# Single blocks moved ahead of the seven-product blocks in a feed-forward trunk on one core

## The chip, the core and the metric

The kernel runs on one core of a Trainium2 chip. A core has four compute engines that matter here, each with its own queue worked in order: TensorE (PE in the profile; the loads of its stationary operand are listed as PEld), VectorE (DVE), ScalarE (ACT) and GpSimd (POOL). SyncE (SP) issues DMAs, and POOL issues some too. Matmul results go to PSUM, which has eight banks here, each 128 partitions by 512 fp32 values.

The metric is the device time of one execution in microseconds (us). Before the change it was 1024.64, the median of three runs (1024.53 to 1025.91).

## The reference

A trunk of two layers on x of 256 tokens by 1024 features, all in fp32. Each layer has a feed-forward network (FFN), a mixer and a second FFN, each added to a scaled x and followed by a layer norm:

```python
D_MODEL, SEQ, DEPTH, D_FF = 1024, 256, 2, 2816

def swiglu_ffn(x, w_in, w_out):
    gate, up = jnp.split(x @ w_in, 2, axis=-1)
    return (jax.nn.silu(gate) * up) @ w_out

# layer i:
#   x <- LN(a*x + 0.5*SwiGLU_1(x))
#   x <- LN(a*x + Mixer_{i mod 2}(x))     mixer 0: sparse attention, mixer 1: Mamba-2 SSD
#   x <- LN(a*x + 0.5*SwiGLU_2(x))
```

The change concerns the four FFNs. In the profiled execution the first runs from about 10 to 190 us, the second from 288 to 465, the third from 465 to 640 and the fourth from 833 to 1021; attention and the SSD mixer lie between.

## The kernel before

**Weights.** The weights lie in DRAM in units of 128 x 1024 fp32 values. Class `Weights` brings each through four steps. SP loads it into a buffer `raw` (L240). ACT casts it to `wh`, a form that PE multiplies fast but with fewer bits (L321, in `make`). DVE subtracts it from `raw` to give `wl`, the low half (L349, in `lows`). PE then forms each product from three matmuls, high by high, low by high and high by low (`mm3`, L527 to L529). Some units are sums of two units: DVE adds the two `raw` buffers (L288), or POOL adds them by a DMA that accumulates (L261). `sums` issues these additions, up to two units ahead of what is made. There are ten slots for made units, and `raws` (7 or 9) limits the loaded ones. `pump` makes the next units; with `most` it stops where DVE is already given much work (`debt`).

**An FFN.** The 2816 hidden columns are 22 blocks of 128, worked in three kinds of steps.

- *Wide blocks* (blocks 0 to 3, eight units): x^T times the weights, token half after token half. In the first FFN the second wide block uses the banks `ptr`, elsewhere all use the two banks `pmm`. Beside them run the eight pieces of `xT.sums` (L564 to L579), which form sums of parts of x^T on ACT (L558) and DVE.
- *Seven-product blocks* (`seven(j, outs)`, four columns each, 14 units): seven products instead of eight, in the order A11, Q1, Q4, S2, S3, A12, A22, in banks `pmm` and one `ptr`, with the output units of earlier blocks (12 matmuls into the banks `acc`) between them. Four of its units are weight sums by DVE and four by POOL.
- *Single blocks* (`one(j)`, one column each): the gate half, then the up half, each a `proj_w` of one unit: eight matmuls of 512 columns (L676) and eight of 256 (L678). ACT copies the second half of the bank out (L885), and DVE's add (L886) reads the first half, after which the bank is free. Then come silu (ACT, L896), the product (DVE, L889) and the high and low forms of the result (ACT L891, DVE L892).

For wide and seven-product blocks, `glu` forms silu and product (L772, L775, L778), and `turn` transposes the result on PE (L764, into `pht` or `ptr`); ACT (L765) and DVE (L766) take it out. At the end of an FFN `tail` runs six output units for the first 128 tokens, then for the others, and the layer norms (DVE L610, L621, L623, L630, L634; POOL L517 and L519). The next stage's transposes of x (L545) follow them.

The order on each engine is the order in which the program emits the instructions. `later(f, d)` puts a piece of work off by d steps; `step` works off these pieces and then pumps units. What stands ahead of a piece in an engine's queue is thus set by where the steps lie. `ffn_plan` names the steps of an FFN: 'S' are seven-product blocks with the output units that run in them, 'R' the single blocks, and the last list is the tail's output units.

Of the kernel before, what the change touches and what calls it, by code (L numbers as in the profile page):

```python
# [63 lines left out]
MOST = 2500  # L64


def ffn_plan():


    s = [(4, [[0], [1], [2], [3]]), (8, [[6], [7], [4], [5]]), (12, [[10], [11], [8], [9]]),  # L70
         (16, [[14], [15], [12], [13]])]
    return [('S', *a) for a in s] + [('R', 20, []), ('R', 21, [])], [16, 17, 18, 19, 20, 21]


def ffn_units(ws, wi, wo, wide):
# [125 lines left out]
class Weights:  # L201
# [158 lines left out]
            self.make()  # L360
            n -= 1

    def pump(self, n=1, now=False, most=None):


        now = now or not self.defer
        if not now:
            self.lows()
        while n and self.made < self.n and self.made < self.done + self.slots:
            if most is not None and self.debt > most and self.made > self.done + 5:  # L370
                break
            self.make()
            n -= 1
        if now:
            self.lows()
        else:
            self.sums()
# [28 lines left out]
def trunk_kernel(ctx: ExitStack, tc: tile.TileContext, widths, forms, x, ln_g, ln_b, wts, kvg, convp,  # L406
# [22 lines left out]
    def f1(s):  # L429
        return wk.tile([128, 256], F32, name=nm(s), tag="f1", bufs=6)  # L430

    def r2(s):
        return wk.tile([128, 512], F32R, name=nm(s), tag="r2", bufs=10)
# [7 lines left out]
    def pmm():  # L441
        return psum.tile([128, 512], F32, name=nm("pmm"), tag="pmm", bufs=2)
# [11 lines left out]
    def ptr():  # L454
        return psum.tile([128, 512], F32, name=nm("ptr"), tag="ptr", bufs=2)

    W = Weights(nc, f4, ring, wts, widths, forms, SLOTS, RAWS)
# [22 lines left out]
    def warm_up(n):  # L480

        for i in range(n):
            nc.tensor.transpose(warm[:, (i % 4) * 128:(i % 4 + 1) * 128], ident, ident)
# [248 lines left out]
    def ffn(xT, u0, ln_i, first=False, last=False, ff=False):  # L732
# [9 lines left out]
        def later(f, d=1):  # L742

            while len(queue) < d:
                queue.append([])
            queue[d - 1].append(f)

        def items():
            for f in queue.pop(0) if queue else []:
                f()  # L750

        def step(n=2, most=MOST):
            items()
            W.pump(n, most=most)

        ready = {}

# [10 lines left out]
        def glu(t, w, c, sil=None):  # L768


            g, h = (c[:, :256], c[:, 256:]) if sil is None else (sil, f1("h"))
            nc.scalar.activation(g, c[:, :256], AF.Silu)  # L772
            out_of = sil is not None and (w >= WIDE or (t and w and not first))
            if out_of:
                nc.scalar.copy(h, c[:, 256:])  # L775

            def mul():
                nc.vector.tensor_mul(h, h if out_of else c[:, 256:], g)  # L778
                W.owe(800)
                ready.setdefault(w, {})[t] = h  # L780
                if len(ready[w]) == 2:
                    later(lambda: later(turn(w, ready.pop(w))), 2)

            later(mul)

        def wide(t, w, ps, k0, k1):
            proj_a(ps, xT, t, u + 4 * w, 512, 2, t == 1, k0, k1)

        if first:
            W.make(between=lambda: xT.fill(0, [0]))  # L790
            warm_up(WARM)
            xT.fill(1, [0])
            for w in range(WIDE):
                ps = [ptr(), ptr()] if w else [pmm(), pmm()]
                for k in range(0, DK, 2):
                    for t in range(2):
                        if (w, k, t) == (0, 0, 1):
                            W.pump(1, now=True)
                        if (w, k) == (0, 2):
                            xT.fill(t, [1])  # L800
                            W.pump(1 + 2 * t, now=True)
                        if (w, k, t) == (0, 4, 1):
                            W.pump(3, now=True)
                        wide(t, w, ps[t], k, k + 2)
                    if w:
                        items()
                        W.pump(1, now=True)
                for t in range(2):
                    glu(t, w, ps[t], f1("sil"))
                if not w:  # L810
                    for i in range(8):
                        later(lambda i=i: xT.sums(i), 1 + i // 2)
        else:
            for t in range(2):
                for w in range(WIDE):
                    ps = pmm()
                    if t:
                        for k in range(0, DK, 2):
                            wide(t, w, ps, k, k + 2)
                            if k % 4:  # L820
                                W.product()
                            if k + 2 < DK:
                                step(1)
                            W.defer = True
                    else:
                        wide(t, w, ps, 0, 5)
                        items()
                        if w == WIDE - 1:
                            W.lows()
                            xT.fill(1)  # L830
                            for i in range(8):
                                later(lambda i=i: xT.sums(i), 1 + i)
                        wide(t, w, ps, 5, DK)
                        items()
                    glu(t, w, ps, f1("sil"))
                    if t:
                        step(1)
# [32 lines left out]
        def one(j):  # L870

            nonlocal u
            bank = pmm if j % 2 == 0 else ptr
            if j % 2 == 0:
                hH[j // 2], hL[j // 2] = r2("hH"), r2("hL")
            H, L = [a[j // 2][:, (j % 2) * 256:(j % 2 + 1) * 256] for a in (hH, hL)]
            g, h = f1("gate"), f1("h")

            def half(o):
                nonlocal u  # L880
                ps = bank()
                proj_w(ps, xT, u)
                W.product()
                u += 1
                nc.scalar.copy(o, ps[:, SEQ:])  # L885
                return lambda: nc.vector.tensor_add(o, ps[:, :SEQ], o)  # L886

            def mul():
                nc.vector.tensor_mul(h, h, g)  # L889
                W.owe(1400)  # L890
                later(lambda: nc.scalar.copy(H, h))  # L891
                later(lambda: nc.vector.tensor_sub(L, h, H.bitcast(F32)), 2)  # L892

            later(half(g))
            step(most=None)
            later(lambda: nc.scalar.activation(g, g, AF.Silu))  # L896
            later(half(h))
            later(mul, 2)
            step(most=None)

        def seven(j, outs):

# [797 lines left out]

    xT = XT(True)
    u, xT = ffn(xT, 0, 0, first=True)
    u, xT = attention(xT, u, 1)
    u, xT = ffn(xT, u, 2, ff=True)
    u, xT = ffn(xT, u, 3)
    u, xT = ssd(xT, u, 4)
    u, _ = ffn(xT, u, 5, last=True)
# [36 lines left out]
```

## Time and profile before

| | us |
|---|---|
| median of three runs | 1024.64 |
| profiled execution | 1022.81 |
| its span | 1021.1 |
| PE busy | 1004.0 (98%) |
| DVE busy | 907.6 (89%) |
| ACT busy | 661.6 (65%) |
| DVE's subtractions `wl`, L349 | 494.9 in 423 |
| ACT's casts `wh`, L321 | 429.9 in 430 |
| DVE's weight sums, L288 | 76.8 in 64 |

Busy time of PE is the time in which any matmul is in the pipe, and matmuls overlap: a matmul of 512 columns is listed with 0.39 us, though in a dense stretch one starts every 0.23. In a timeline the number in front is the start from the beginning of the span, and the second one is the duration; `x8` says that the row stands for eight instructions. What stands in brackets is idle time ahead of the instruction and what ended it.

### The profile page before, as it was taken

What the parts mean: (1) busy time and instruction counts of PE and PEld (TensorE: products, weight loads), DVE (VectorE), ACT (ScalarE), POOL (GpSimd) and SP (SyncE); (2) the same over time, 40 slices, a digit from 0 to 9 for tenths busy, and PEclk for the clock granted to TensorE, in tenths of its full rate; (3) what the DMA queues carried; (4) which work ended last, traced back from release to release, by engine and by line L of the source; (5) the groups of instructions that cost most, each with busy time, mean ns of one, the idle gap of its engine ahead of it and who ended that gap; (6) DMA issues with size and microseconds to landing.
All of it is one profiled execution on the core that took longest, in us unless ns stands there. A gap on an engine that the chain in (4) does not pass through costs nothing.

```text
span 1021.1 us, 14624 instructions
## 1 busy us (share of the span) xinstructions
PE 1004.0 (98%) x5279; PEld 847.8 (83%) x5279; DVE 907.6 (89%) x1264; ACT 661.6 (65%) x965; POOL 121.4 (12%) x179
## 2 busy tenths in 40 slices
PE   8999999999999999999999999999999999999996
PEld 7788888888787888888888888999899888888885
DVE  6899998789789999988999998788999978999985
ACT  6666775477656667764676775486876645777760
POOL 2101100100011011001110100150111110101101
PEclk9999999999999999999999999999999999999998
DMA  9899999352547899992789999358765654999861
GB/s 334 219 287 277 294 262 350 116 155 94 187 144 170 266 285 293 255 374 88 183 271 275 299 265 338 127 174 240 208 216 188 198 202 108 279 273 252 256 235 41
DMA packets 64665, 231.70 MB, mean 227 GB/s; under 512 B 7280, under 2 KB 7344, under 8 KB 64592
## 3 DMA queue, kind: packets, MB, share of 16 engines
q1 hardware_dynamic: 51264, 183.43, 49.2%
q0 software_dynamic: 13040, 46.82, 23.6%
q8 instruction: 41, 0.67, 0.3%
q10 hardware_dynamic: 288, 0.52, 0.1%
q14 instruction: 32, 0.26, 0.1%
HBM read 193.48 MB, written 1.08 MB: 191 GB/s over the span
## 4 chain that ended last, share of the span: by engine, by line
PE 79%; DVE 11%; DMA 4%; issue 3%; ACT 2%; POOL 1%; SPq 0%; POOLq 0%; DVEq 0%; ACTq 0%
PE pmm L529 10%; PE pmm L527 10%; PE pmm L528 10%; PE acc L527 9%; PE acc L529 9%; PE acc L528 9%; DVE wl L349 4%; DVE raw L288 2%; DMA raw<-raw 2%; PE pxs L527 2%; PE pxs L529 2%; PE pxs L528 2%; PE pmm L676 1%; PE ptr L676 1%; PE ptr L527 1%
## 5 line engine op out<-in xcount | busy, mean ns | idle before, releaser
L349 DVE TENSOR_TENSOR wl<-raw,wh 128x1024 fp32r<-128x1024 f32 (+2 forms) x423 | 494.9, 1212 | 11.1 <-ACT wh L321 10.3
L321 ACT CAST wh<-raw 128x1024 fp32r<-128x1024 f32 (+3 forms) x430 | 429.9, 1045 | 109.8 <-DVE raw L288 52.0
L527 PE MATMUL acc<-wh,hH 128*128 128x512 f32 (+1 forms) x352 | 137.8, 392 | 0.0
L528 PE MATMUL acc<-wl,hH 128*128 128x512 f32 (+1 forms) x352 | 136.6, 388 | 0.7 <-DVE wl L349 0.7
L529 PE MATMUL acc<-wh,hL 128*128 128x512 f32 (+1 forms) x352 | 136.8, 389 | 0.3 <-DVE hL L766 0.2
L527 PE MATMUL pmm<-wh,xT 128*128 128x512 f32 (+2 forms) x320 | 125.8, 393 | 0.0
L529 PE MATMUL pmm<-wh,xT 128*128 128x512 f32 (+2 forms) x320 | 123.4, 386 | 0.1
L528 PE MATMUL pmm<-wl,xT 128*128 128x512 f32 (+2 forms) x320 | 122.9, 384 | 0.0
L261 POOL DMA_DIRECT2D raw<-raw x64 | 55.4, 865 | 448.3 <-DVE raw L288 250.2
L528 PE MATMUL pmm<-wl,xf 128*128 128x512 f32 x256 | 100.2, 391 | 1.5 <-DVE wl L349 1.5
L527 PE MATMUL pmm<-wh,xf 128*128 128x512 f32 x256 | 100.4, 392 | 0.4
L529 PE MATMUL pmm<-wh,xf 128*128 128x512 f32 x256 | 99.8, 390 | 0.0
L529 PEld LDWEIGHTS acc<-wh,hL 128*128 128x128 f32 x352 | 66.1, 188 | 14.9 <-DVE hL L766 1.2
L528 PEld LDWEIGHTS acc<-wl,hH 128*128 128x128 f32 x352 | 66.2, 188 | 14.1 <-DVE wl L349 1.1
L288 DVE TENSOR_TENSOR raw<-raw,raw 128x1024 f32<-128x1024 f32 x64 | 76.8, 1217 | 0.2
L527 PEld LDWEIGHTS acc<-wh,hH 128*128 128x128 f32 x352 | 66.2, 188 | 12.8
L529 PEld LDWEIGHTS pmm<-wh,xT 128*128 128x128 f32 x320 | 60.2, 188 | 13.5 <-DVE xT L524 1.4
L528 PEld LDWEIGHTS pmm<-wl,xT 128*128 128x128 f32 x320 | 60.3, 189 | 11.1 <-DVE wl L349 0.3
L527 PEld LDWEIGHTS pmm<-wh,xT 128*128 128x128 f32 x320 | 60.4, 189 | 10.5
L528 PEld LDWEIGHTS pmm<-wl,xf 128*128 128x128 f32 x256 | 48.1, 188 | 12.7 <-DVE wl L349 3.0
L527 PEld LDWEIGHTS pmm<-wh,xf 128*128 128x128 f32 x256 | 48.1, 188 | 11.4 <-ACT h L775 1.6
L529 PEld LDWEIGHTS pmm<-wh,xf 128*128 128x128 f32 x256 | 48.1, 188 | 10.0
(315 smaller groups left out, 1778.2 us busy)
## 6 DMA issues: line engine op xcount, KB each, us to landing
raw<-in_wts_dram SPq DMA_DIRECT2D x339, 512.0 KB, 5.9
raw<-raw POOLq DMA_DIRECT2D x64, 512.0 KB, 6.0
M<-scr POOLq DMA_DIRECT2D x8, 512.0 KB, 5.5
lng<-in_ln_g_dram POOLq DMA_DIRECT2D x6, 512.0 KB, 5.7
lnb<-in_ln_b_dram POOLq DMA_DIRECT2D x6, 512.0 KB, 7.0
wl<-raw POOLq DMA_DIRECT2D x5, 512.0 KB, 5.5
raw<-in_wts_dram SPq DMA_DIRECT2D x4, 408.0 KB, 6.0
out_dram<-x SPq DMA_DIRECT2D x4, 256.0 KB, 2.1
```

What stands on the lines that cost most here:

```text
L261: self.nc.gpsimd.dma_start(self.raw[r], self.raw[other], accum_op=ALU.add)
L288: self.nc.vector.tensor_add(self.raw[r], self.raw[r], self.raw[other])
L321: nc.scalar.copy(h[:, c:c + n], raw[:, c:c + n])
L349: self.nc.vector.tensor_sub(lo[:, s], raw[:, s], h[:, s].bitcast(F32))
L527: nc.tensor.matmul(ps, lh, rh, start=first, stop=False, skip_group_check=on)
L528: nc.tensor.matmul(ps, lh, rl, start=False, stop=False, skip_group_check=on)
L529: nc.tensor.matmul(ps, ll, rh, start=False, stop=last, skip_group_check=on)
L676: nc.tensor.matmul(ps, H[:, k * 128:(k + 1) * 128], xT.HL[:, k, :], start=k == 0, stop=False)
```

## The change

The plan of all four FFNs puts the two single blocks right behind the wide blocks, where they are columns 4 and 5; the seven-product blocks start at columns 6, 10, 14 and 18, and the last of these now runs with 7 raw buffers instead of 9. Both single blocks use the banks `pmm`. In their steps no unit is made whose weight sum hasn't been issued (`plain`), and the limit `most` holds there, which it didn't. In the first FFN the pieces of `xT.sums` are put one to a step instead of two.

```diff
 def ffn_plan():
-    s = [(4, [[0], [1], [2], [3]]), (8, [[6], [7], [4], [5]]), (12, [[10], [11], [8], [9]]),
-         (16, [[14], [15], [12], [13]])]
-    return [('S', *a) for a in s] + [('R', 20, []), ('R', 21, [])], [16, 17, 18, 19, 20, 21]
+    s = [(6, [[0], [1], [2], [3]]), (10, [[4], [5], [8], [9]]), (14, [[6], [7], [12], [13]]),
+         (18, [[10], [11], [16], [17]])]
+    return [('R', 4, []), ('R', 5, [])] + [('S', *a) for a in s], [14, 15, 20, 21, 18, 19]
...
-    def pump(self, n=1, now=False, most=None):
+    def pump(self, n=1, now=False, most=None, plain=False):
...
             if most is not None and self.debt > most and self.made > self.done + 5:
                 break
+            if plain and self.forms[self.made][1] is not None and self.summed <= self.made:
+                break
             self.make()
...
-        def step(n=2, most=MOST):
+        def step(n=2, most=MOST, plain=False):
             items()
-            W.pump(n, most=most)
+            W.pump(n, most=most, plain=plain)
...
                 if not w:
                     for i in range(8):
-                        later(lambda i=i: xT.sums(i), 1 + i // 2)
+                        later(lambda i=i: xT.sums(i), 1 + i)
...
         def one(j):
-            bank = pmm if j % 2 == 0 else ptr
+            bank = pmm
...
             later(half(g))
-            step(most=None)
+            step(plain=True)
             later(lambda: nc.scalar.activation(g, g, AF.Silu))
             later(half(h))
             later(mul, 2)
-            step(most=None)
+            step(plain=True)
```

Line numbers behind `pump` are two higher in the changed kernel (L349 and L288 stay, L886 becomes L888). The first place to look at is DVE's queue in the second FFN where the wide blocks end. Before the change it holds, from the low half of the transposed result of the first wide block on (`hL_392`):

```order
L766 TENSOR_TENSOR hL_392_3023<-pht_417_3180,hH_391_3022 128x512
L349 TENSOR_TENSOR wl128_3187<-raw_379_2948,wh128_3186 128x1024
L778 TENSOR_TENSOR h_419_3208<-h_419_3208,sil_418_3207 128x256
L349 TENSOR_TENSOR wl129_3199<-raw_385_2984,wh129_3198 128x1024
L288 TENSOR_TENSOR raw_370_2880<-raw_370_2880,raw_390_3016 128x1024
L349 TENSOR_TENSOR wl130_3216<-raw_390_3016,wh130_3215 128x1024
L288 TENSOR_TENSOR raw_379_2948<-raw_379_2948,raw_399_3072 128x1024
L349 TENSOR_TENSOR wl131_3261<-raw_399_3072,wh131_3260 128x1024
```

At the same place the changed kernel has the adds of the single blocks (L888). `gate_426` and `h_427` belong to the first single, in the banks `pmm_428` and `pmm_431`, and `gate_434` to the second, in `pmm_436`. From the last product of the wide blocks (`h_423`) on:

```order
L780 TENSOR_TENSOR h_423_3224<-h_423_3224,sil_422_3223 128x256
L349 TENSOR_TENSOR wl131_3212<-raw_385_2984,wh131_3211 128x1024
L888 TENSOR_TENSOR gate_426_3231<-pmm_428_3233,gate_426_3231 128x256
L888 TENSOR_TENSOR h_427_3232<-pmm_431_3262,h_427_3232 128x256
L349 TENSOR_TENSOR wl132_3257<-raw_390_3016,wh132_3256 128x1024
L349 TENSOR_TENSOR wl133_3260<-raw_411_3143,wh133_3259 128x1024
L288 TENSOR_TENSOR raw_385_2984<-raw_385_2984,raw_416_3162 128x1024
L288 TENSOR_TENSOR raw_390_3016<-raw_390_3016,raw_418_3177 128x1024
L891 TENSOR_TENSOR h_427_3232<-h_427_3232,gate_426_3231 128x256
L768 TENSOR_TENSOR hL_394_3025<-ptr_432_3280,hH_393_3024 128x512
L888 TENSOR_TENSOR gate_434_3300<-pmm_436_3302,gate_434_3300 128x256
```

The add into `gate_434` has moved here from the end of the FFN, and two units' `wl` and two weight sums stand between it and the add before. On ACT the same stretch of the changed kernel reads as follows; L887 are the copies out of the singles' banks, L777 the one out of the last wide bank.

```order
L321 CAST wh131_3211<-raw_385_2984 128x1024
L774 ACTIVATE sil_422_3223<-pmm_417_3167 128x256
L777 COPY h_423_3224<-pmm_417_3167 128x256
L887 COPY gate_426_3231<-pmm_428_3233 128x256
L321 CAST wh132_3256<-raw_390_3016 128x1024
L321 CAST wh133_3259<-raw_411_3143 128x1024
L887 COPY h_427_3232<-pmm_431_3262 128x256
```

Two of these casts, `wh131` and `wh132`, take a `raw` buffer that a weight sum on DVE has written, and the copies stand behind them.

The second place is DVE's queue at the end of the second FFN, from the product `h` of the last seven-product block to the first add of the layer norm (L610, L612 in the changed kernel). Before, with the singles in between (the second half of these rows):

```order
L349 TENSOR_TENSOR wl205_4400<-raw_522_4252,wh205_4399 128x1024
L349 TENSOR_TENSOR wl206_4403<-raw_523_4276,wh206_4402 128x1024
L886 TENSOR_TENSOR h_540_4406<-ptr_544_4439,h_540_4406 128x256
L349 TENSOR_TENSOR wl207_4434<-raw_524_4278,wh207_4433 128x1024
L349 TENSOR_TENSOR wl208_4437<-raw_527_4302,wh208_4436 128x1024
L892 TENSOR_TENSOR hL_532_4338<-h_534_4340,hH_531_4337 128x256
L889 TENSOR_TENSOR h_540_4406<-h_540_4406,gate_539_4405 128x256
L892 TENSOR_TENSOR hL_532_4338<-h_540_4406,hH_531_4337 128x256
L349 TENSOR_TENSOR wl209_4467<-raw_529_4330,wh209_4466 128x1024
L349 TENSOR_TENSOR wl210_4470<-raw_530_4332,wh210_4469 128x1024
L610 SCALAR_TENSOR_TENSOR x0_71<-acc_432_3273,x0_71 128x512
```

After, all of them:

```order
L780 TENSOR_TENSOR h_538_4406<-h_538_4406,sil_537_4405 128x256
L349 TENSOR_TENSOR wl203_4391<-raw_529_4312,wh203_4390 128x1024
L349 TENSOR_TENSOR wl204_4415<-raw_530_4314,wh204_4414 128x1024
L349 TENSOR_TENSOR wl205_4418<-raw_531_4335,wh205_4417 128x1024
L768 TENSOR_TENSOR hL_519_4174<-ptr_540_4432,hH_518_4173 128x512
L768 TENSOR_TENSOR hL_517_4172<-ptr_543_4447,hH_516_4171 128x512
L349 TENSOR_TENSOR wl206_4445<-raw_533_4360,wh206_4444 128x1024
L349 TENSOR_TENSOR wl207_4460<-raw_534_4362,wh207_4459 128x1024
L349 TENSOR_TENSOR wl208_4463<-raw_535_4386,wh208_4462 128x1024
L349 TENSOR_TENSOR wl209_4466<-raw_536_4388,wh209_4465 128x1024
L349 TENSOR_TENSOR wl210_4469<-raw_539_4412,wh210_4468 128x1024
L612 SCALAR_TENSOR_TENSOR x0_71<-acc_448_3402,x0_71 128x512
```

Eight units' `wl` and two `hL` stand between the product and the layer norm's add, and no row of a single block.

## The prediction

> **What bounds the kernel now.** I read the page first: the shares of the engines, then the chain that ended last.
>
> ```profile
> span 1021.1 us, 14624 instructions
> PE 1004.0 (98%) x5279; PEld 847.8 (83%) x5279; DVE 907.6 (89%) x1264; ACT 661.6 (65%) x965; POOL 121.4 (12%) x179
> PE 79%; DVE 11%; DMA 4%; issue 3%; ACT 2%; POOL 1%; SPq 0%; POOLq 0%; DVEq 0%; ACTq 0%
> ```
>
> PE is busy for 98% of the span and carries 79% of the chain, so the change can only take back time in which PE waits. DVE, at 89%, is the engine it waits for. It has little slack, so where its work lies in its queue decides. The profiled execution took 1022.81 us, 1.7 more than its span and 1.83 under the median of 1024.64. My sum is made against 1022.81 and the difference then added to the median.
>
> A seven-product block does the same PE work each time it runs (14 weight units and 4 output units), so its length, from the first product of one block to that of the next, is a gauge of loss. I asked for the windows between these starts: for the first FFN blocks 4 and 8, and for FFN 2, 3 and 4 the two blocks 4 and 8 each. The columns are the window, its length, then the busy time of PE, PEld, DVE, ACT and POOL, the granted clock, DMA share and GB/s.
>
> ```profile
> 31.09:64.88 33.79, 31.66 (x142) 25.24 (x140) 31.84 (x36) 22.90 (x32) 3.46 (x4) 1.00 0.87 260
> 64.88:95.76 30.88, 30.88 (x144) 25.56 (x142) 29.59 (x31) 21.96 (x31) 3.47 (x4) 1.00 0.92 273
> 314.01:345.23 31.22, 31.10 (x141) 25.38 (x140) 28.28 (x30) 21.38 (x30) 1.70 (x2) 1.00 0.84 260
> 345.23:376.75 31.52, 31.33 (x144) 25.41 (x142) 30.55 (x33) 23.25 (x33) 4.29 (x5) 1.00 0.91 265
> 491.16:522.36 31.20, 31.08 (x141) 25.39 (x140) 28.36 (x30) 21.45 (x30) 1.78 (x3) 1.00 0.84 259
> 522.36:553.75 31.39, 31.28 (x143) 25.40 (x142) 30.45 (x33) 23.19 (x33) 4.20 (x5) 1.00 0.92 266
> 859.46:890.69 31.23, 31.11 (x142) 25.39 (x140) 28.82 (x31) 21.92 (x31) 2.25 (x3) 1.00 0.82 259
> 890.69:921.61 30.92, 30.92 (x144) 25.48 (x141) 29.98 (x33) 22.52 (x33) 3.75 (x5) 1.00 0.92 271
> ```
>
> A block without a wait takes 30.88 us. The first FFN's first block loses 33.79 − 30.88 = 2.91. The six rows of the later FFNs add up to 187.48, which is 2.20 over 6 × 30.88 = 185.28. PE's timeline shows the large hole of the first FFN, and the waits of the weight loads show a smaller one ahead of the blocks.
>
> ```profile
> 40.96 0.39 PE L527 MATMUL pmm<-wh,xf 128*128 128x512 f32 x1
> 42.38 0.50 PE L528 MATMUL pmm<-wl,xf 128*128 128x512 f32 x1 [1.03 <-DVE wl L349]
> 42.72 0.40 PE L529 MATMUL pmm<-wh,xf 128*128 128x512 f32 x1
> PEld pht L764 <- DVE h L778: 1.0, 3, 0.3
> ```
>
> The hole is DVE's: the low half `wl` of a weight unit is late, because the sums of x^T and of the weights stand ahead of it. The last row is a stall of 0.3 in each of three places, the transposes `pht` in the wide blocks of FFN 2 to 4, which wait for the product `h`: 0.9 in all. So 2.9 + 2.2 + 0.9 = **6.0 us** are there to be won in these places.
>
> **The change part by part.** No engine gets an instruction more or less; everything is order.
>
> *First FFN.* The two single blocks (four products) now stand between the wide and the seven-product blocks. The sums of x^T are spread over eight steps instead of four. These rows give what a single costs:
>
> ```profile
> 435.43 0.39 PE L527 MATMUL acc<-wh,hH 128*128 128x512 f32 x1
> 438.15 0.60 PE L764 MATMUL ptr<-ident,c 128*128 128x128 f32 x4
> 444.62 2.00 PE L676 MATMUL ptr<-xT,wh 128*128 128x512 f32 x8
> 447.41 2.00 PE L676 MATMUL ptr<-xT,wh 128*128 128x512 f32 x8
> ```
>
> An output unit (12 matmuls) takes 438.15 − 435.43 = 2.72 of PE. The half of a single, which also uses up one unit, takes 447.41 − 444.62 = 2.79. The singles thus give DVE four times 2.79 of PE work, 11.2 us, in which to get the sums done. Following the new order of DVE row by row with the durations below, I find each `wl` of the first block ready before PE gets there; the smallest margin is about 0.45. Cover for this is the 11.2 us themselves. If it were used up, the old 2.9 would come back. I take **−2.9**, between 0 and −2.9.
>
> *FFN 2 to 4: what goes.* In the wide blocks DVE no longer does two weight sums ahead of `h`, so the 0.3 before `pht` goes. The lost 2.2 should go for the same reason as in the first FFN. I take **−3.1** together, between 0 and −3.1.
>
> *FFN 2 to 4: what comes.* All four halves of the singles now write to the two banks `pmm`, where the second single had the banks `ptr`. So the second single waits until DVE has added up the first one, and the first product of block 6 waits for the second single's first half (the add into `gate` at L886). That add is one row in DVE's queue, behind two weight sums. The rows that price the queue:
>
> ```profile
> 306.31 1.28 DVE L561 TENSOR_TENSOR xf<-xq,xf 128x512 fp32r<-128x512 f32 x2
> 307.97 0.39 ACT L772 ACTIVATE sil<-pmm 128x256 f32<-128x256 f32 x1 [0.43 <-PE pmm L529]
> 310.51 0.42 DVE L778 TENSOR_TENSOR h<-pmm,sil 128x256 f32<-128x256 f32 x1
> 310.84 1.22 DVE L349 TENSOR_TENSOR wl<-raw,wh 128x1024 fp32r<-128x1024 f32 x1
> 314.42 2.00 ACT L321 CAST wh<-raw 128x1024 fp32r<-128x1024 f32 x2
> 318.47 1.22 DVE L288 TENSOR_TENSOR raw<-raw,raw 128x1024 f32<-128x1024 f32 x1
> 319.60 1.22 DVE L349 TENSOR_TENSOR wl<-raw,wh 128x1024 fp32r<-128x1024 f32 x1
> ```
>
> From start to start, a row of 256 columns costs DVE 0.34, a weight unit or a weight sum 1.14, and a row of 512 about 0.61. A CAST costs ACT 0.95. I start from the silu at 307.97, whose input is PE's own and so comes at the same time in both kernels. `h` follows at 308.44. The 14 rows from there through the first add into `gate` are five `wl` and two weight sums (7 × 1.14), three rows of 256 (1.02) and four of 512 (2.44, and 0.1 for one that waits for ACT): 11.5, so that add ends near 320.0. The add into `h` behind it waits for ACT's copy. The copy stands behind two CASTs, and the first of these waits for the second weight sum, which ends one `wl` and two rows of 256 before 320.0, at 318.2; two CASTs and the copy later (1.9 + 0.4) it is 320.5, and the add ends near 320.9. Then come two `wl`, two weight sums, two rows of 256 and one of 512, 4 × 1.14 + 2 × 0.34 + 0.61 = 5.9: the bank is free near **326.9**, and the product can start at 327.0.
>
> PE would be there earlier. Block 4 started at 314.01; less the 0.3 of the stall before `pht` the wide blocks end near 313.7. Four halves and one set of transposes (0.45, from 444.62 back to the end of the half before) make 11.6, so PE wants the bank at 325.3. The wait is **1.7** in each of three FFNs, 0.35 of it already at the second single: **+5.1**. The same rows bound it: nothing if DVE's queue runs 1.7 ahead of my count, 2.8 if one row of 1.14 more lands ahead of the add. FFN 3 and FFN 4 repeat FFN 2's order and, by the windows above, its phase within 0.05, so I multiply by three.
>
> The Trainium skill speaks against this part of the change: "Perfetto Trace Analysis", section "Optimizing Tensor Performance", has independent matmul groups rotate through different PSUM banks, so that the eviction of one overlaps the matmuls of the next. By that rule the sum is the one with the wait, and no run shown so far has singles on two banks alone.
>
> *Tails.* Before, the singles stood ahead of the tail and DVE idled in them. Now the last block runs straight into it.
>
> ```profile
> 436.31 0.42 DVE L778 TENSOR_TENSOR h<-h,sil 128x256 f32<-128x256 f32 x1 [0.22 <-ACT h L775]
> 436.65 3.49 DVE L349 TENSOR_TENSOR wl<-raw,wh 128x1024 fp32r<-128x1024 f32 x3
> 440.06 0.68 DVE L766 TENSOR_TENSOR hL<-ptr,hH 128x512 fp32r<-128x512 f32 x1
> 450.20 0.40 PE L527 MATMUL acc<-wh,hH 128*128 128x512 f32 x1
> 457.25 0.68 DVE L610 SCALAR_TENSOR_TENSOR x<-acc,x 128x512 f32<-128x512 f32 x1
> 176.25 0.69 DVE L610 SCALAR_TENSOR_TENSOR x<-acc,x 128x512 f32<-128x512 f32 x1 [0.36 <-PE acc L529]
> 634.24 0.69 DVE L610 SCALAR_TENSOR_TENSOR x<-acc,x 128x512 f32<-128x512 f32 x1 [1.04 <-PE acc L529]
> 463.22 0.75 DVE L634 SCALAR_TENSOR_TENSOR x<-x,rs,lnb 128x512 f32<-128x512 f32 x1
> 463.83 1.03 PE L545 MATMUL pxT<-ident,x 128*128 128x128 f32 x8
> ```
>
> In FFN 2, DVE has after `h` at 436.31 eight `wl` and two `hL` to do before the layer norm's first add: 0.34 + 8 × 1.135 + 2 × 0.65 puts it at 447.05. PE is done for that add 457.25 − 450.20 = 7.05 into its tail, which now starts at 438.15 + 0.9 of transposes: 446.1. DVE is 0.9 late, and the transposes of the normed x follow DVE at once (463.22 to 463.83), so PE gets it: **+0.9**. In FFN 1 the add waited 0.36 for PE, which leaves **+0.5**. In FFN 3 it waited 1.04: nothing. Behind FFN 4 no units follow: nothing. The tails thus cost 1.4, between 0 and 1.8 (0.9 in both).
>
> *The rest.* The stop before a unit without its sum, and the other numbers of the output units, move CASTs and loads among steps. SP's and POOL's transfers keep their number, and the raw buffers keep enough loads ahead that none is the last wait in my count: nothing.
>
> **Sum:** −2.9 − 3.1 + 5.1 + 1.4 = +0.5, so 1023.3 for the profiled execution and **1025.1** for the median.
>
> **Rivals.** *The bank is free in time.* If ACT and DVE run ahead of my count by 1.7, the wait isn't there: −2.9 − 3.1 + 1.4 = −4.6, **1020.0**. For it: PE's later matmuls forgive a late `wl`, and my queue is a hand count of some 22 rows. Against it: no gap in these rows that could be closed up, and all durations are of this trace.
>
> *ACT holds the first single's bank.* This is the slower side. The second half of the first single reuses the last wide bank, which ACT frees with a copy behind a CAST that waits for a weight sum on DVE. I find the bank free at 316.4 to 316.5, and PE there at 316.5. From that point each delay of DVE goes to PE here, and the later banks move along. A single row of 1.14 more ahead of that sum gives 1.1 in each of three FFNs: +3.3, **1028.4**.
>
> *The singles give no pause in FFN 2 to 4.* There DVE works without a gap through them, so the blocks behind may lose their 2.2 as before: **1027.3**. Against it: PE's own wait of 1.7 lets DVE catch up.
>
> *The clock drops in the new holes.* The trace shows a slow start:
>
> ```profile
> 1.42 2.39 PE L483 MATMUL ptr<-ident 128*128 128x128 f32 x10 [1.42 <-POOL ident masks.py:199]
> 6.53 1.06 PE L545 MATMUL pxT<-ident,x 128*128 128x128 f32 x4
> ```
>
> Four transposes take 1.06 there against 0.60 at 438.15. If each new hole brought on such a stretch of half pace (1.42 to 7.6, worth 3.1), it would be +9.3: **1034**. Against it: behind the hole of 1.03 at 42.38 the matmuls run at full pace, and that window's clock is 1.00. The Trainium skill's "TensorE: Matmul & The Clock Gate", section "A second HAM failure mode: psum-queue depth-cycling", has such a drop where PE idles a little at every change of banks. The trace does not bear it out.
>
> **How the numbers follow.** I give the forecast 0.45, the free bank 0.24, ACT's copy 0.19, no pause 0.09, the clock 0.03. A measurement of this kernel can tell about 0.2%, 2 us. The free bank and a sliver of the forecast are faster: 0.26. Most of the forecast is the same: 0.40. The rest is slower: 0.34. The range runs from a little under the free bank to a little over ACT's copy, 1019.6 to 1028.9; the forecast's own is 1023.5 to 1026.8.
>
> **What would show it.** Right: the first block of the first FFN at 30.9 (block 6 now); in FFN 2 to 4 a PE wait ahead of block 6's first product, put down to DVE's add into `gate`, 1.3 long, and 0.35 at the second single; the blocks at 30.9; the layer norm's first add 0.9 late in FFN 2. Wrong: no wait on `pmm` there (the first rival), a wait on ACT's copy of `h` (the second), blocks at 31.2 to 31.5 (the third), a granted clock under 1.00 (the fourth).

## The result and the profile after

The changed kernel takes **1033.89 us** (median of four runs, 1033.39 to 1034.59) against 1024.59 for the kernel before: 0.9% slower, ratio 1.0089 with a 95% interval of 1.0071 to 1.0106. The time lies outside the range. The profiled executions, 1022.81 and 1034.59, lie 11.8 us apart, 2.5 more than the medians, since the one is below the other runs of its kernel (1024.40 to 1025.91) and the other is the longest of its four. The terms below are read from these two and add up to 11.8. One execution of run 3 below was in a slow state (1108.63 us, granted clock 0.849) and is left out of its median.

The page of the changed kernel, span, engines and chain:

```profile
span 1032.9 us, 14622 instructions
PE 1008.2 (98%) x5279; PEld 848.1 (82%) x5279; DVE 907.1 (88%) x1264; ACT 662.6 (64%) x965; POOL 121.5 (12%) x179
PE 53%; DVE 21%; issue 11%; DMA 9%; ACT 3%; POOL 1%; POOLq 0%; DVEq 0%; ACTq 0%
```

The engines run the same matmuls, casts and sums, but the chain has moved: PE's share of it falls from 79% to 53%, DVE's rises from 11% to 21%, the DMAs' from 4% to 9%, and issue (time in which the profile shows no wait) from 3% to 11%. PE waits for others more often. Where, the windows of the changed kernel tell. First come the singles and the first block of the first FFN, then the singles and the four blocks of FFN 2, then the last two blocks of FFN 3 and of FFN 4 (columns as in the prediction).

```profile
31.45:43.04 11.59, 11.59 (x70) 10.26 (x69) 11.52 (x18) 7.03 (x13) 1.80 (x2) 1.00 0.61 193
43.04:73.34 30.30, 30.30 (x138) 25.09 (x137) 29.52 (x34) 20.74 (x31) 2.58 (x3) 1.00 0.86 260
312.71:326.01 13.30, 12.15 (x70) 10.29 (x68) 12.74 (x17) 7.98 (x15) 1.81 (x2) 1.00 0.67 154
326.01:356.44 30.43, 30.43 (x136) 25.18 (x137) 26.24 (x30) 19.92 (x27) 3.42 (x4) 1.00 0.81 233
356.44:387.32 30.88, 30.88 (x143) 25.56 (x142) 27.65 (x29) 19.65 (x25) 2.58 (x3) 1.00 0.82 257
387.32:419.18 31.86, 31.64 (x143) 25.32 (x142) 27.05 (x30) 21.25 (x28) 2.58 (x3) 1.00 0.87 251
419.18:452.31 33.13, 31.91 (x147) 25.84 (x146) 32.10 (x36) 25.80 (x35) 3.93 (x5) 1.00 0.89 262
568.72:600.89 32.17, 31.61 (x144) 25.32 (x142) 27.52 (x30) 21.23 (x28) 2.58 (x3) 1.00 0.87 250
600.89:634.03 33.14, 31.90 (x147) 25.84 (x146) 31.26 (x35) 25.72 (x35) 3.44 (x4) 1.00 0.90 253
941.70:973.50 31.80, 31.62 (x143) 25.33 (x142) 27.09 (x30) 21.24 (x28) 2.58 (x3) 1.00 0.85 245
973.50:1006.66 33.16, 31.92 (x147) 25.84 (x146) 32.11 (x36) 25.72 (x35) 4.54 (x6) 1.00 0.81 234
```

The stall of the first FFN is gone (30.30). The singles take 13.30 in FFN 2 and 11.59 in the first FFN, so 1.7 is waiting (FFN 3 and 4 take 13.33 and 13.31). The first two blocks of FFN 2 are clean, and so are those of FFN 3 and 4 (30.43 and 30.88 each). The third should take 30.88 and the last 31.32, as they do in the first FFN and in the fastest experiments (the last one holds the transposes before the tail, which stood among the singles before). They lose 0.98 + 1.81 in FFN 2, 1.29 + 1.82 in FFN 3 and 0.92 + 1.84 in FFN 4: **8.7 us**, which the prediction doesn't have. The clock is 1.00 in all these windows.

The tails of FFN 1, 2 and 3, each from its first matmul to a fixed place in the next stage, in the kernel before:

```profile
169.22:208.13 38.91, 38.77 (x210) 32.85 (x208) 30.44 (x48) 17.94 (x29) 5.59 (x9) 1.00 0.50 167
450.20:487.67 37.47, 37.47 (x175) 30.82 (x173) 33.71 (x47) 15.89 (x24) 4.05 (x6) 1.00 0.48 153
627.21:665.60 38.39, 38.39 (x223) 33.98 (x222) 29.17 (x40) 17.39 (x28) 5.50 (x10) 1.00 0.53 183
```

and in the changed kernel:

```profile
166.42:207.05 40.63, 39.31 (x210) 32.83 (x208) 33.02 (x49) 20.65 (x31) 6.16 (x10) 1.00 0.63 229
452.31:490.89 38.58, 37.89 (x175) 30.82 (x174) 34.91 (x47) 19.89 (x27) 3.20 (x6) 1.00 0.69 252
634.03:673.45 39.42, 38.78 (x223) 33.99 (x222) 31.44 (x40) 19.41 (x29) 6.07 (x11) 1.00 0.64 227
```

They cost 1.7, 1.1 and 1.0 more. FFN 4's tail, which runs to the end of the program, costs 0.2 more.

Where PE waits inside a block is best followed upstream. PE's timeline in FFN 2's last block:

```profile
423.20 0.50 PE L530 MATMUL pmm<-wl,xf 128*128 128x512 f32 x1 [0.80 <-DVE wl L349]
```

DVE is late with this `wl` because it idled in the third block:

```profile
411.42 0.69 DVE L924 TENSOR_TENSOR c<-c 128x512 f32<-128x512 f32 x1 [3.11 <-ACT c L947]
```

ACT's timeline of the same stretch:

```profile
405.43 1.05 ACT L321 CAST wh<-raw 128x1024 fp32r<-128x1024 f32 x1 [0.50 <-DMA raw<-raw]
409.86 1.05 ACT L321 CAST wh<-raw 128x1024 fp32r<-128x1024 f32 x1 [3.37 <-DMA raw<-raw]
410.82 0.58 ACT L947 COPY c<-pmm 128x512 f32<-128x512 f32 x1
```

ACT's copy of product S3 (L947) comes behind a CAST that waits 3.37 us for a weight sum, which POOL makes by a DMA (`raw<-raw`). DVE needs the copy and waits 3.11 us. In the first FFN, and in the kernel before at the same step, the copy stands ahead of that CAST. ACT's timeline in the kernel before, in the third block of FFN 2:

```profile
396.59 0.59 ACT L945 COPY c<-pmm 128x512 f32<-128x512 f32 x1 [1.69 <-PE pmm L529]
398.47 2.01 ACT L321 CAST wh<-raw 128x1024 fp32r<-128x1024 f32 x2 [1.29 <-DMA raw<-raw]
```

The difference of one place comes from the singles, in whose steps FFN 2 to 4 make more units ahead than the first FFN. Counted along ACT's queue of the changed kernel, FFN 2 has three CASTs more ahead of the copy of S3 than the first FFN has in the first block, two more in the second, one more in the third and none in the last; FFN 3 and 4 have the same. In the second block a CAST that waits for such a sum stands ahead of the copy as well, but it waits only 1.89: the copy starts 21.0 behind the block's start, and the block is clean. In the third block the copy starts 23.5 behind it.

A smaller wait of the same kind lies at that block's start. The second block's last copy (`h`, L777) stands behind the CAST of a unit that DVE has just summed. ACT's timeline, then DVE's:

```profile
387.83 1.05 ACT L321 CAST wh<-raw 128x1024 fp32r<-128x1024 f32 x1 [2.37 <-DVE raw L288]
389.06 0.36 ACT L777 COPY h<-pmm 128x256 f32<-128x256 f32 x1
```

```profile
389.46 0.43 DVE L780 TENSOR_TENSOR h<-h,sil 128x256 f32<-128x256 f32 x1 [1.38 <-ACT h L777]
```

### The profile page after: what moved, and what is told of

Its sections match the earlier page's. It is cut to its first block, busy times and chain, and to the rows that moved or that the text cites. A ratio compares the mean times of both kernels' runs of the same rounds, so it can differ in the third digit from the quotient of the medians.

```text
span 1032.9 us, 14622 instructions
## 1 busy us (share of the span) xinstructions
PE 1008.2 (98%) x5279; PEld 848.1 (82%) x5279; DVE 907.1 (88%) x1264; ACT 662.6 (64%) x965; POOL 121.5 (12%) x179
## 4 chain that ended last, share of the span: by engine, by line
PE 53%; DVE 21%; issue 11%; DMA 9%; ACT 3%; POOL 1%; POOLq 0%; DVEq 0%; ACTq 0%
DVE wl L349 12%; DMA raw<-raw 7%; PE pmm L531 7%; PE pmm L529 7%; PE pmm L530 7%; PE acc L529 5%; PE acc L531 5%; PE acc L530 5%; DVE raw L288 3%; ACT wh L321 2%; DMA raw<-in_wts_dram 2%; PE pxs L529 1%; PE pxs L531 1%; PE pxs L530 1%; PE ptr L1541 1%
## 5 line engine op out<-in xcount | busy, mean ns | idle before, releaser
L349 DVE TENSOR_TENSOR wl<-raw,wh 128x1024 fp32r<-128x1024 f32 (+2 forms) x423 | 495.1, 1213 | 20.2 <-ACT wh L321 19.8
L288 DVE TENSOR_TENSOR raw<-raw,raw 128x1024 f32<-128x1024 f32 x64 | 77.1, 1220 | 0.5
```

What stands on the lines that cost most here:

```text
L288: self.nc.vector.tensor_add(self.raw[r], self.raw[r], self.raw[other])
L349: self.nc.vector.tensor_sub(lo[:, s], raw[:, s], h[:, s].bitcast(F32))
```

## The experiments

Each is an edit of the changed kernel (1033.9) unless said otherwise. Three theories stood at the start: Q, that CASTs of sums hold up the copies behind them on ACT; B, that the last block lacks raw buffers; C, that the bank wait itself displaces the later work. The bank wait is the 1.7 in the singles. The ratios are to the kernel before, run beside each; lines that only hand a parameter on or fit a slice are left out below (`...`).

**1. The second single in `ptr`.**

```diff
-            bank = pmm
+            bank = pmm if j % 2 == 0 else ptr
```

> The second single block gets the banks ptr back; everything else is the changed kernel's. Three theories of the 9.3 us. (Q, queue) The singles of FFN 2 to 4 make units too far ahead, so that in the third seven-product block ACT's copy of S3 stands behind a CAST that waits for POOL's weight sum: DVE is late after it and the last two blocks lose. (B, buffers) The last block loses because it runs with 7 raw buffers instead of 9. (C, bank) The wait on pmm displaces DVE's work against PE, and the later losses are its echo. Bank wait itself: by all three the stretch from the first single to the next block shrinks from 13.3 to about 11.7 us in each of FFN 2 to 4, 4.8 in all. Q and B: the last two blocks stay at 31.8 to 32.2 and 33.1, so 1029. C: they return to 30.9 and 31.3, so 1020 to 1021.

Measured: 1048.34, ratio 1.0228 (1.0210 to 1.0246). All three theories missed: the singles got longer, 17.47 in FFN 2 and 13.58 instead of 11.59 in the first FFN. PE's waits of this kernel (us in total, times, longest):

```profile
PE ptr L678 <- DVE hL L768: 11.7, 3, 3.9
```

and three rows of its windows, the singles, the third and the last block of FFN 2:

```profile
314.53:332.00 17.47, 13.56 (x69) 11.57 (x68) 14.98 (x18) 7.19 (x12) 1.81 (x2) 0.90 0.55 132
393.19:426.41 33.22, 31.49 (x143) 25.35 (x142) 29.21 (x32) 21.19 (x29) 2.58 (x3) 1.00 0.86 250
426.41:459.32 32.91, 31.93 (x147) 25.84 (x146) 31.86 (x36) 25.84 (x35) 3.94 (x5) 1.00 0.89 264
```

The banks `ptr` are no freer than `pmm`: the transposes of the second wide block hold one until DVE has taken `hL` out, and that row stands behind the same two `wl` and two weight sums. So the wait of 0.9 becomes one of 3.9, three times. At this place of the program the banks `pmm` are the better choice. The last two blocks keep their losses, but since the bank wait grew instead of going, this run doesn't test C; runs 5 and 9 do.

**2. Fewer units ahead.**

```diff
-            step(plain=True)
+            step(1 if not first else 2, plain=True)
```

(in both places of `one`)

> In FFN 2 to 4 each step of a single block makes at most one unit instead of two; the banks stay pmm. Q: the order settles as in the first FFN, the last two blocks of FFN 2 to 4 go back to 30.9 and 31.3 (2.8 us in each FFN, 8.5 in all), and the time falls to about 1025.5, or a little less if the bank wait shrinks as well. B: the last block stays at 33.1, 1034. C: the bank wait of 1.6 stays and so do the losses, 1034.

Measured: **1021.82**, ratio 0.9971 (0.9962 to 0.9981), 0.3% faster than the kernel before and 3.7 us below the 1025.5 expected. Its windows, the singles, the third and the last block of FFN 2:

```profile
312.60:324.85 12.25, 11.98 (x70) 10.34 (x68) 11.05 (x15) 6.57 (x11) 1.81 (x2) 1.00 0.58 128
386.04:416.92 30.88, 30.88 (x144) 25.56 (x141) 29.58 (x31) 21.97 (x31) 3.44 (x4) 1.00 0.93 271
416.92:448.23 31.31, 31.31 (x147) 26.00 (x145) 29.95 (x33) 24.18 (x33) 3.08 (x4) 1.00 0.94 274
```

As Q has it, the 8.7 are gone in all three FFNs, and the bank wait shrank from 1.7 to 0.65 as well: only the second single's wait of 0.27 is left, none ahead of block 6. That makes the other 3 us. As both went together, this run alone doesn't tell Q from C.

**3. Nine raw buffers.**

```diff
-            W.raws = 9 if j < 18 else 7
+            W.raws = 9
```

> Nine raw buffers in the last seven-product block and the tail too. B: the last block of FFN 2 to 4 goes from 33.1 back to 31.3, 1.8 us each, so about 1028.5. Q and C: less than 0.5 us of change, 1033.5 to 1034.5.

Measured: 1034.68, the median of three runs, ratio 1.0099 (1.0072 to 1.0126). The last block of FFN 2 and FFN 3 still takes 32.90 and 33.02. B falls.

**4. One single ahead of the blocks, one ahead of the tail**, in all FFNs; the output units are dealt out to suit, and the seven raw buffers hold for the last block and the single behind it.

```diff
...
-    return [('R', 4, []), ('R', 5, [])] + [('S', *a) for a in s], [14, 15, 20, 21, 18, 19]
+    return [('R', 4, [])] + [('S', *a) for a in s] + [('R', 5, [])], [15, 20, 21, 18, 19, 5]
...
```

> One single block stays ahead of the seven-product blocks, the other goes back between the last of them and the tail, in all four FFNs. The tails of the changed kernel cost 1.7, 1.1, 1.0 and 0.2 us more than before. If that is because no single gives DVE time ahead of the tail, 3 to 4 us of it goes. Q: the third block of FFN 2 to 4 has its copy ahead of the CAST again, so the last two blocks are at 30.9, 8.5 less, but the first two may lose 0.3 to 1. Sum by Q 1021 to 1024; by B 1029; with the tails' cost from elsewhere 3 more in each.

Measured: 1029.85, ratio 1.0046 (1.0031 to 1.0060), worse than all of Q's sum. The first two blocks of the first FFN and the tail of FFN 2:

```profile
39.59:71.65 32.06, 31.30 (x140) 25.42 (x141) 30.47 (x34) 21.63 (x29) 2.60 (x3) 1.00 0.86 260
71.65:103.24 31.59, 31.38 (x144) 25.40 (x142) 30.61 (x33) 23.26 (x33) 4.33 (x5) 1.00 0.92 276
453.68:493.22 39.54, 37.98 (x175) 30.73 (x174) 34.71 (x47) 19.28 (x27) 2.60 (x4) 1.00 0.60 213
```

With one single the first two blocks of the first FFN lose 1.2 and 0.7 against 30.88, and a single ahead of the tail doesn't make the tail shorter (39.54 against 38.58). One single's pause is thus not enough; whether two would do, as before the change, this run doesn't show. Q missed a part here too: the last block has no loss, but the third takes 31.89, 31.63 and 31.64 in FFN 2 to 4 instead of 30.88, which I did not follow up.

**5 and 9. One CAST, then two, behind the copies.** Run 5 makes one unit less in one step of the third block of FFN 2 to 4. The CAST that waits for POOL's sum then stands behind the copy of S3, and nothing else changes place but its own `wl`. Run 9 also makes no unit in one step of the second block, which moves one CAST behind that block's last silu and copy.

```diff
-            out()        # ahead of S3
+            out(1 if j == 14 and not first else 2)
...
-            out()        # ahead of A22, run 9 only
+            out(0 if j == 10 and not first else 2)
```

> The changed kernel with one CAST less made ahead of product S3 in the third seven-product block of FFN 2 to 4: the CAST that waits for POOL's weight sum now stands behind ACT's copy of S3, one place later in ACT's queue (its subtraction on DVE one place later too), in three places of the program. Banks, singles, loads and everything else are the changed kernel's. Q: DVE's wait of 3.1 us for that copy goes to below 1, the third and the last block of FFN 2 to 4 go back to 30.9 and 31.3, and the time falls by 8 us to about 1026. A rival (P, pause): the last blocks lose since DVE has more work ahead than before, and the order of this one CAST doesn't matter: blocks stay at 31.8 to 33.1, 1033 to 1034.

> As the run in which the CAST in the third block stands behind the copy of S3, and besides the CAST of the third unit of that block stands behind ACT's silu and copy of the second block's last product (A22) in FFN 2 to 4, two places later in ACT's queue; nothing moves on DVE. Q (a CAST that waits for a weight sum holds up the copy behind it, and with it DVE): DVE's wait of 1.4 for that copy goes, the third block of FFN 2 to 4 falls from 31.75, 32.2 and 31.4 to 30.9, 2.7 us in all, and the time from 1028.3 to about 1025.6. P (what DVE has ahead, whatever the order): no change, 1028.

Measured: 1028.32, ratio 1.0033 (1.0018 to 1.0048), and 1025.37, ratio 1.0007 (0.9997 to 1.0017). The third and the last block of FFN 2, then of FFN 3, with one CAST moved:

```profile
387.84:419.59 31.75, 31.18 (x144) 25.48 (x142) 29.66 (x32) 22.68 (x32) 3.44 (x4) 1.00 0.86 257
419.59:450.90 31.31, 31.31 (x147) 25.99 (x146) 29.95 (x33) 24.07 (x33) 3.09 (x4) 1.00 0.95 282
567.29:599.52 32.23, 31.52 (x144) 25.35 (x142) 30.12 (x33) 22.67 (x32) 3.44 (x4) 1.00 0.88 256
599.52:630.84 31.32, 31.32 (x148) 25.99 (x146) 29.95 (x33) 24.20 (x33) 3.09 (x4) 1.00 0.93 272
```

and the third block of FFN 2 and of FFN 3 with two moved:

```profile
387.23:418.11 30.88, 30.88 (x143) 25.56 (x142) 29.52 (x32) 22.13 (x30) 3.44 (x4) 1.00 0.88 261
565.78:597.34 31.56, 31.17 (x143) 25.48 (x142) 30.36 (x33) 22.11 (x30) 3.44 (x4) 1.00 0.89 262
```

The first CAST is the whole loss of the last block, 1.8 in each FFN. I had expected the third block to follow it as well; it didn't, but it followed the second CAST. In FFN 4 the two blocks take 31.40 and 31.32 in run 5, 30.88 and 31.32 in run 9. Of the 8.7 us, 8.0 are gone with two CASTs moved (the medians differ by 8.5). The bank wait stays (13.33, 13.34 and 13.30 for the singles in run 9), so C falls, and so does the rival of run 5's expectation, that the order of the CASTs doesn't matter. This settles Q. In FFN 3 the third block keeps 0.7, which I did not follow up.

**6. No limit and no stop in the singles' steps.**

```diff
-            step(plain=True)
+            step(most=None)
```

> The singles' steps pump without the limit most and without the stop before a unit that has no sum, as before the change; the rest is the changed kernel. Eight units are then ahead at the first seven-product block of FFN 2 to 4 instead of six. Q: the CAST still stands ahead of the copy of S3 in the third block, so the last two blocks keep their loss of 2.8; in the first FFN and the bank wait something between nothing and 2 us more, since more CASTs and weight sums stand ahead of the adds. 1034 to 1040. If the stop itself cost the time (units made too late), it would be faster than 1034 by more than 2.

Measured: 1034.86, ratio 1.0109 (1.0090 to 1.0128). The sum hides two large terms. In the first FFN the singles take 13.91 instead of 11.59 and the first block 33.77 instead of 30.30: 5.8 lost to new bank waits (holes of 2.16 and 1.75) and to a lower clock behind the first of them (0.95 in that block; see the last section). In FFN 2 to 4 the third block is at 30.88 and the last at 31.7 to 32.1, 6.8 won. The expectation had the first, not the second. The stop and the limit are thus what protects the first FFN.

The second shows how the two CASTs work together. The CAST still stands ahead of the copy of S3 in the third block, as expected. ACT's row in FFN 2, then DVE's:

```profile
413.17 1.05 ACT L321 CAST wh<-raw 128x1024 fp32r<-128x1024 f32 x1 [2.25 <-DMA raw<-raw]
414.73 0.69 DVE L924 TENSOR_TENSOR c<-c 128x512 f32<-128x512 f32 x1 [1.36 <-ACT c L947]
```

It waits 2.25 instead of 3.37 and DVE 1.36 instead of 3.11, and the last block loses 0.4 to 0.8 instead of 1.8. The other CAST doesn't hold up `h` here: DVE has no wait of 1.38 at the third block's start, and POOL issues the sum 11.8 behind that start instead of 13.1. The copy starts 21.3 behind it, as early as in the clean second block. So a place in the queue costs as much as the sum is late, and the wait at the block's start seems to make the later one longer; that this is the whole difference is not shown.

**7. The sums of x^T two to a step.**

```diff
-                        later(lambda i=i: xT.sums(i), 1 + i)
+                        later(lambda i=i: xT.sums(i), 1 + i // 2)
```

(in the first FFN)

> The pieces of the sums of x^T in the first FFN two to a step again, the rest is the changed kernel. If the two singles alone give DVE the time, the first FFN stays as it is (first block at 30.3): 1033 to 1034.5. If the spacing is what removed the 2.9, up to 2.9 come back: 1036.5.

Measured: 1032.89, ratio 1.0084 (1.0068 to 1.0100), the first block at 30.31. The spacing does nothing; the singles, with their stop and limit, remove the stall.

**8, 10, 11 and 12. The tails**, all on top of run 2 (1021.8). Run 8 keeps the next stage's `wl` back until the first layer norm is issued. Run 10 has two of them made by ACT and an accumulating DMA of POOL, the first two of each tail; run 11 takes the last two instead (units 92, 93, 209, 210). Run 12 adds to run 11 that in FFN 1 one `wl` of the tail stands behind the two `hL` on DVE.

```diff
...
-        W.lows()
+        W.lows(max(W.made - (u + len(ks)), 0))      # run 8, in tail
...
-        self.by_dma = set()
+        self.by_dma = {92, 93, 209, 210}            # run 11; run 10 {90, 91, 207, 208}
...
-            out()
+            out_pieces(outs.pop(0), 1 if first and j == 18 else 0)   # run 12: one wl kept back
...
```

> The faster kernel with at most one unit per step in the singles of FFN 2 to 4 (1021.8), and in the tail DVE makes only the low halves of the tail's own units ahead of the first layer norm; those of the next stage follow behind it. If the eight units ahead of the layer norm's first add are what makes it late, the tails of FFN 1 and 2 lose 0.6 to 1.0 less each (the group of transposes of x at 0.8 instead of 1.6 in FFN 2), about 1020.3. If the next stage needs its low halves as early as that, it gives the gain back at its first products, 1021 to 1023.

> The faster kernel with at most one unit per step in the singles of FFN 2 to 4 (1021.8). The low halves of the first two units behind FFN 1 and FFN 2 are made by ACT (negated copy) and an accumulating DMA of POOL instead of DVE, so that six units instead of eight stand ahead of the layer norm's first add. If DVE's queue there is what makes the tails late, the transposes of x in FFN 2 take 0.8 instead of 1.6 and FFN 1's tail gets 0.2 to 0.4 shorter: 1020.5 to 1021. If the tails' cost comes from elsewhere (ACT, the low half hL, loads), 1021.5 to 1023.

> As the run with two low halves behind FFN 1 and FFN 2 made by ACT and POOL's accumulating DMA, but of the last two units made ahead of the layer norm instead of the first two, so that ACT's extra copies stand behind all four CASTs and hold up no subtraction of DVE. If DVE's queue of eight units makes FFN 2's tail late, the layer norm's first add comes 1.1 us earlier there, and the tail gets 0.9 shorter; FFN 1's tail 0.2 to 0.4: 1020.5 to 1021 against 1021.8 for the kernel with fewer units ahead. If not DVE's queue but something behind it sets the tail, no change, 1021.5 to 1022.5.

> As the run beside it, and in the first FFN one subtraction of the tail's own units stands behind the two low halves hL instead of ahead of them on DVE. The wait of PE for hL in that tail (0.5 to 1.1 us by DVE's late hL, the group of 60 matmuls at 14.4 to 15.1 instead of 13.6) shrinks by 0.5 to 1.0: 0.5 to 1 us less than the run beside it, about 1020. If hL waits for ACT and not for its turn on DVE, no change.

Measured: 1041.77 (ratio 1.0163, 1.0142 to 1.0183), 1022.49 (0.9970, 0.9960 to 0.9981), 1020.26 (0.9965, 0.9952 to 0.9977) and **1020.17** (0.9960, 0.9946 to 0.9974). Run 8 lies far above both branches of its expectation: its kept units come between the layer norm and the low half of the next x^T, and PE waits for that:

```profile
PE pmm L531 <- DVE xT L526: 14.9, 4, 4.5
```

Run 10 gains nothing: ACT's extra copies stand ahead of the last CASTs, and in FFN 2 DVE waits 2.91 for one of these, so the layer norm's first add comes later than without the edit. Run 11 frees DVE. In the changed kernel's timeline the first add of the layer norm in FFN 2 waits for nothing but its turn on DVE, 8.18 behind the tail's start:

```profile
460.49 0.68 DVE L612 SCALAR_TENSOR_TENSOR x<-acc,x 128x512 f32<-128x512 f32 x1
```

In run 11's timeline it comes 7.56 behind the start and waits for PE again:

```profile
456.20 0.69 DVE L612 SCALAR_TENSOR_TENSOR x<-acc,x 128x512 f32<-128x512 f32 x1 [1.37 <-PE acc L531]
```

The window of FFN 2's tail in run 11:

```profile
448.64:486.65 38.01, 37.85 (x176) 30.83 (x175) 33.07 (x45) 21.69 (x29) 5.34 (x8) 1.00 0.86 290
```

The tail of FFN 2 goes from 38.55 in run 2 to 38.01, less than the 0.9 expected, because a late `hL` now holds PE for 0.4. Run 12 takes the same wait out of FFN 1's tail, which goes from 40.16 in run 11 to this:

```profile
166.32:205.34 39.02, 38.91 (x211) 32.85 (x209) 31.15 (x47) 22.00 (x33) 7.35 (x11) 1.00 0.76 254
```

Against run 11 the medians don't show it (0.1 us); the window of this one profile does, in which FFN 3's tail is 0.9 longer than in run 11's. Both are faster than both kernels, by about 4 us against the kernel before.

## Why the prediction was wrong

| term | predicted | in the two profiles |
|---|---|---|
| first FFN's stall | −2.9 | −2.8 |
| what goes ahead of and in the first two blocks of FFN 2 to 4 | −3.1 | −3.3 |
| bank wait in FFN 2 to 4 | +5.1 | +5.2 |
| third and last block of FFN 2 to 4 | 0 | **+8.7** |
| tails | +1.4 | +4.0 |
| sum | +0.5 | +11.8 |

The first term is read from where the first tail starts, 166.42 instead of 169.22. Between the tails FFN 2 to 4 are 10.5 longer in all, of which the bank wait is 5.2 and the last two blocks 8.7; the −3.3 is what remains.

*What held.* The first three terms came out as worked. The stall of the first FFN went, and run 7 shows that the singles do it without the wider spacing. The bank wait is in the places that the prediction names, put down to DVE's add:

```profile
319.25 2.12 PE L678 MATMUL pmm<-xT,wh 128*128 128x512 f32 x8 [0.26 <-DVE gate L888]
326.01 0.50 PE L529 MATMUL pmm<-wh,xT 128*128 128x512 f32 x1 [0.89 <-DVE gate L888]
```

The listed holes of 0.26 and 0.89 are less than the 1.7 lost, since a matmul is listed to its end (0.39) though in a dense stretch the next one starts after 0.23, and behind the second hole the next start takes 0.33 (326.01 to 326.34). By run 2, where only the first hole is left and 0.65 is lost, the split is near 0.65 and 1.05, where the prediction had 0.35 and 1.3: the sum is right by some luck in its parts. Two details of the working don't change it: the rows up to the free bank add up to 326.8, not 326.9, and the add at 457.25 waited for its turn on DVE, not for PE; that PE is done 7.03 into the tail is in the rows of FFN 1 and FFN 3.

*What failed.* The step is the term "The rest", put at nothing: that the stop before a unit without its sum and the other numbers of the output units only "move CASTs and loads among steps". The prediction checked there whether loads suffice and didn't check where CASTs land among the copies on ACT. The term measures +8.7. With it fell "the blocks at 30.9". A block's loss was taken to be fixed where DVE falls behind, so I followed DVE's queue row by row as far as the first block and took the rest as steady. But the surplus of units made in the singles carries over from block to block, one less in each, and in the third the CAST of a sum that comes late stands ahead of the copy of S3. Runs 5 and 9 put 8.0 of the 8.7 on two CASTs in each FFN.

*The rival that was near.* "ACT holds the first single's bank" has the right mechanism, a copy behind a CAST that waits for a weight sum, at the wrong place and with a price of 3.3 instead of 8.7. The free bank fell with the wait. The clock rival's 1034 is the measured time by chance: the clock did not drop. "The singles give no pause" fell too: the first two blocks take 30.43 and 30.88.

*The tails* were right in kind and too small. FFN 2 has 1.1 against 0.9, and run 11 shows that DVE's eight `wl` are what the layer norm waits for. FFN 1 has 1.7 against 0.5: the layer norm's first add comes 8.83 behind the tail's start, against 7.03 before, because DVE is 1.3 us later there than I had it, and PE waits 1.09 for `hL`, which I didn't look at; run 12 takes 1.1 of it back. FFN 3's 1.0, where the prediction had nothing, is again PE waiting for `hL` (0.64 at 636.75). It stands so in this profile and in run 12's; most others have 38.5 to 38.6, against 38.39 before. Why DVE is late with `hL` in these two stays open.

*The rule that was weighed.* The Trainium skill ("Perfetto Trace Analysis", "Optimizing Tensor Performance") would rotate matmul groups through different banks. Run 1 has four banks instead of two for the singles, and is 14.5 us slower, so here the measurement decides: a bank more helps only if its last reader comes early in its own queue.

## What to carry to other kernels

On an engine that works in order, a conversion whose input is still being summed is a wait for everything behind it; put the copies that other engines need ahead of it, or don't issue it yet. When a change moves work between stages, count what each stage hands to the next (here, units made ahead), and follow the order through every repeat of the loop until the count is steady: the first two repeats can be clean and the third not. And before giving a product another bank, look at who reads that bank last and what stands ahead of that reader.

## What the hardware showed that I had not expected

The clock rival was priced from the start of the program, and run 1 shows it in the middle. Behind its hole of 3.91 us the clock is at half, and eight matmuls take 3.68 us instead of the 2.09 that the same eight take at 320.59, ahead of the hole. The row of PE's timeline:

```profile
327.53 3.68 PE L678 MATMUL ptr<-xT,wh 128*128 128x512 f32 x8 [3.91 <-DVE hL L768]
```

and the window behind it (the clock is the third number from the end):

```profile
328.00:330.00 2.00, 2.00 (x6) 1.52 (x6) 2.00 (x2) 0.00 (x0) 0.00 (x0) 0.50 0.03 8
```

By these two rows the half clock costs 1.6 us beside the wait. The Trainium skill ("TensorE: Matmul & The Clock Gate", "What's actually happening") puts the drop after an idle window of about 3.4 us, which this hole agrees with. In run 6 the clock dropped behind a hole of 2.16, shorter than that figure: the hole ends at 45.64, from 47.20 on the matmuls start every 0.43 us, and the clock from 48 to 50 is 0.50.

```profile
45.64 0.50 PE L529 MATMUL pmm<-wh,xT 128*128 128x512 f32 x1 [2.16 <-DVE gate L888]
47.63 0.63 PE L530 MATMUL pmm<-wl,xT 128*128 128x512 f32 x1
48.05 0.63 PE L531 MATMUL pmm<-wh,xT 128*128 128x512 f32 x1
```

In the changed kernel's windows above, with holes of 0.9, the clock stays at 1.00.
